# Squares, scalings and final outputs moved between engines and places in a two-layer mLSTM and attention encoder

## Chip, cores and metric

The kernel runs on one core of one Trainium2 chip. Its time is the device time of one execution in microseconds. Three runs gave a median of 1946.82 us (1946.59 to 1949.53). All tensors are float32.

## What is computed

Two sequences, a prompt of 256 tokens and a sample of 512, go through the same trunk of two layers at width 1024, each with its own conditioning vector c. In the reference, cut to what matters here:

```python
for l in range(2):
    sh1, sc1, g1, sh2, sc2, g2 = split(silu(c) @ adaln_w[l] + adaln_b[l], 6)
    h = rmsnorm(x, norm_g[l, 0]) * (1 + sc1) + sh1
    y = mlstm_mixer(h, ...) if l == 0 else swa_mixer(h, ...)
    x = x + g1 * y
    h = rmsnorm(x, norm_g[l, 1]) * (1 + sc2) + sh2
    x = x + g2 * conv_ffn(h, ...)
return rmsnorm(x, final_g)          # rmsnorm(x, g) = x * rsqrt(mean(x*x) + eps) * g

# in mlstm_mixer, for each of 4 heads (256 columns):
hs = h_fwd + h_bwd                  # two scans over the sequence, in opposite directions
hs = hs * rsqrt(mean(hs * hs, axis=-1) + eps) * head_g
```

The mLSTM projects h to queries, keys, values, output gates and 16 gate columns (an input and a forget gate for each head and direction); the attention of layer 1 looks at a window of 128 tokens to each side with a bias and a sink; the feed-forward has a convolution of width 3 and a width of 2816.

## The kernel before

**Layout.** The 768 tokens are columns: 0 to 256 the prompt, 256 to 768 the sample. The 1024 features are eight chunks of 128 partitions. A matrix product is made of three matmuls: both operands are split into a high part, rounded to the matmul's fast format, and a low part, the rest (`fp_copy_split`, L218 to L226: high part by ScalarE, low part by VectorE), and high x high, low x high and high x low are added. So each weight block `raw` that a DMA brings (five buffers) becomes `whi` and `wlo` (three buffers each), and each activation `hh` and `hl` (in the tiles `zh` and `zl`).

**Start.** `first` (L1241 on) loads the sample in two halves of 256 tokens (the first two of `RANGES`), sums squares and scales them by the root (`scaled`, L482 to L485), while PE multiplies adaLN rows to get shift and gain. When these are there, `modulate` (L487 to L494) multiplies each of the eight chunks of each half by the gain and adds the shift, in place, by a GpSimd instruction (L491), and splits it. Then `mlstm` loads the prompt and starts its norm (L576 to L579): eight squares on ScalarE (L102), all but the last two added up by GpSimd (L106), a matmul with a vector of 1/1024 on PE that sums over the partitions (L118), add and power (VectorE L120, GpSimd L123), a broadcast on PE (L128), and then, in `modulated` (L466 on), product (VectorE L474), high part (ScalarE L476) and low part (VectorE L477). Meanwhile `window` (L273 on) multiplies the gates' block and the first two query blocks with the two sample halves and then the prompt.

**Order.** The Python code states an order, in which `tick` and `step` interleave norms and adaLN work between the products; a scheduler of the framework then sets each engine's final order. An engine runs its own queue in order. From the start on, VectorE also works on layer 1's adaLN (`adaln_v`: L431, L433, on rows that come through the same five `raw` buffers).

**Gates and heads.** After the window, VectorE scans the gates over time (L590 to L597); the rows go through DRAM (L599, L615), GpSimd adds masks (L617), ScalarE takes exponentials (L676 to L680), VectorE multiplies them into the scores (L681, L682). For each head and sequence, the outputs `hs` (128 tokens x 256) are summed from two directions (L725, L726), squared with an accumulated sum (L728), the root is taken (VectorE L730, GpSimd L731), GpSimd multiplies `hs` by it (L734), PE transposes it (L738) and VectorE applies `head_g` (L742). There are 24 such blocks: 4 heads times 4 blocks of the sample and 2 of the prompt.

**End.** The last step of the second feed-forward goes over the three ranges (two halves of the sample, then the prompt). For each it makes eight output tiles of six matmuls in four rotating banks `pa`, adds each to the residual (VectorE L507), squares the result (ScalarE L102) and ticks (L1208), which lets the norm of the range before advance between the tiles. The last norm's `output` (L496 to L501) writes x times the root times `final_g` to a new tile `nt` (eight buffers, which the squares share) and starts a DMA of each chunk to the result.

Of the kernel before, what the change touches and what calls it, by code (L numbers as in the profile page):

```python
# [12 lines left out]
AF = mybir.ActivationFunctionType  # L13
ALU = mybir.AluOpType

P = 128
D = 1024
KC = D // P
# [4 lines left out]
SAMPLE, PROMPT = (256, 768, 0), (0, 256, 1)  # L23
RANGES = ((256, 512, 0), (512, 768, 0), PROMPT)
# [23 lines left out]
FG = HG + 8  # L48
# [26 lines left out]
def col(t):  # L75

    return t + (GAP if t >= 256 else 0)
# [7 lines left out]
class Norm:  # L85

    def __init__(self, net, xt, rng, apply, pool_adds=True):
        self.net, self.xt, self.rng, self.apply = net, xt, rng, apply  # L90
        self.n = rng[1] - rng[0]
        self.sums = []
        self.add = net.nc.gpsimd.tensor_tensor if pool_adds else net.nc.vector.tensor_tensor

    def x(self, c):
        return self.xt[c // 4][:, c % 4, self.rng[0] : self.rng[1]]

    def square(self, c):

        net = self.net  # L100
        sq = net.tmp([P, self.n])
        net.nc.scalar.activation(sq, self.x(c), AF.Square)  # L102
        self.sums.append(sq)
        if 2 <= len(self.sums) and self.count < KC - 2:
            acc = self.sums[0]
            self.add(acc, acc, self.sums.pop(), ALU.add)  # L106
        self.count += 1

    count = 0
# [28 lines left out]
class Net:  # L138
# [348 lines left out]
    def modulate(self, xt, rng, l, i):  # L487
        c0, c1, q = rng
        for c in range(KC):
            x = xt[c // 4][:, c % 4, c0:c1]  # L490
            self.nc.gpsimd.tensor_scalar(  # L491
                x, x, self.gain[l][i][:, c, q : q + 1], self.mod[l][:, 24 * i + c, q : q + 1], ALU.mult, ALU.add
            )
            self.fp_copy_split(self.hh[:, c, c0:c1], self.hl[:, c, c0:c1], x)  # L494

    def output(self, x, pr, rng):  # L496
        for c in range(KC):
            t = self.tmp([P, rng[1] - rng[0]])
            self.nc.vector.scalar_tensor_tensor(t, x(c), self.cst(FG + c), pr, ALU.mult, ALU.mult)  # L499
            self.nc.sync.dma_start(self.io["y"][:, c, rng[0] : rng[1]], t)  # L500
        return ()  # L501


# [45 lines left out]
    def mlstm(self, pool, gw, xt):  # L549
        nc, io = self.nc, self.io  # L550
# [22 lines left out]
        ws = [(gw, gates)] + [(w, keep(qt0, 0, c)) for c, w in self.halves(U_MIN)]  # L573
        self.load_x(io["x"], RANGES[2:], xt)
        nc.sync.dma_start(self.kct[:, P:], io["kc"][:, P : 3 * P])
        norm = Norm(self, xt, PROMPT, self.modulated(0, 0))  # L576
        for c in range(KC):
            norm.square(c)
        self.start(PROMPT, norm.stages())  # L579
# [30 lines left out]
        for h in range(4):  # L610
# [13 lines left out]
            for i in range(2):  # L624
# [3 lines left out]
                t = self.slab([P, 2, 2, T], R)  # L628
# [30 lines left out]
            for q, (s0, s1) in enumerate(SEQS):  # L659
                n = (s1 - s0) // P  # L660
                for j in range(n):
# [21 lines left out]
                    if q == 0:  # L683
                        t = [pool.tile([P, 640], R, tag="PT", name=self.nm("PT"), bufs=8) for _ in range(2)]
# [14 lines left out]
            ss = pool.tile([P, T6], F32, tag="ss", name=self.nm("ss"), bufs=2)  # L699
            for q, (s0, s1) in enumerate(SEQS):  # L700
                n = (s1 - s0) // P
                self.step(self.fillp, 2)
                hq = []
                for i in range(n):
                    ti = s0 // P + i
                    hs = pool.tile([P, 256], F32, tag="hs", name=self.nm("hs"), bufs=4)
                    hq.append(hs)
                    dn = pool.tile([P, 2], F32, tag="dn", name=self.nm("dn"), bufs=4)
                    out = []
                    for d in range(2):  # L710
                        o = self.pa()[:, :258]
                        js = range(0, i + 1) if d == 0 else range(i, n)
                        for j in js:
                            ph, pl = pts[q, j, d]
                            c0 = (i - j) * P if d == 0 else i * P
                            tj = s0 // P + j
                            self.mm(o, ph[:, c0 : c0 + P], v[:, 0, tj], j == js[0], False)
                            self.mm(o, ph[:, c0 : c0 + P], v[:, 1, tj], False, False)
                            self.mm(o, pl[:, c0 : c0 + P], v[:, 0, tj], False, j == js[-1])
                        nc.scalar.activation(dn[:, d : d + 1], o[:, 256:257], AF.Abs)  # L720
                        out.append(o)
                    em = eT[:, ti, h:36:32]
                    nc.vector.tensor_tensor(dn, dn, em, ALU.max)
                    nc.vector.reciprocal(dn, dn)
                    nc.scalar.activation(hs, out[0][:, :256], AF.Copy, scale=dn[:, 0:1])  # L725
                    nc.vector.scalar_tensor_tensor(hs, out[1][:, :256], dn[:, 1:2], hs, ALU.mult, ALU.add)  # L726
                    sq = pool.tile([P, 256], F32, tag="sq", name=self.nm("sq"), bufs=1)
                    nc.scalar.activation(sq, hs, AF.Square, accum_out=ss[:, ti : ti + 1])  # L728
                t0, t1 = s0 // P, s1 // P
                nc.vector.tensor_scalar(ss[:, t0:t1], ss[:, t0:t1], 1.0 / 256.0, EPS, ALU.mult, ALU.add)  # L730
                nc.gpsimd.tensor_tensor(ss[:, t0:t1], ss[:, t0:t1], self.mhalf[:, : t1 - t0], ALU.pow)  # L731
                for ti in range(t0, t1):
                    hs = hq[ti - t0]
                    nc.gpsimd.tensor_scalar(hs, hs, ss[:, ti : ti + 1], 1.0, ALU.mult, ALU.mult)  # L734
                for c in range(2):
                    pt = self.pa()
                    for ti in range(t0, t1):
                        nc.tensor.transpose(  # L738
                            pt[:, (ti - t0) * P : (ti - t0 + 1) * P], hq[ti - t0][:, c * P : (c + 1) * P], self.ident
                        )  # L740
                    ch = 2 * h + c
                    nc.vector.tensor_scalar(  # L742
                        hsT[ch // 4][:, ch % 4, s0:s1], pt[:, : s1 - s0], self.cst(HG + ch), None, ALU.mult
                    )
# [221 lines left out]
    def combined(self, l, i, pool):  # L966
# [20 lines left out]
        def apply(x, pr, rng):  # L987
            if rng[0] == 0:
                for c in range(KC):
                    full[c] = one(F32)  # L990
                    modulate(full[c], c, x, pr, rng)
                    put((self.B11, self.B21)[c // 4], c % 4, full[c])
                return
# [123 lines left out]
    def ffn(self, l, xt, pool, apply, keep=None):  # L1117
        nc = self.nc
# [61 lines left out]
        def down(p, g):  # L1180
            ws = (w for _, w in self.halves(u0 + 3 * p + 2))
            chunk = lambda w, i: [t[:, 512 * i : 512 * (i + 1)] for t in w]

            def tile(w, c, rng):
                s0, s1, _ = rng
                o = self.pa()[:, : s1 - s0]
                cs = slice(c % 4 * P, (c % 4 + 1) * P)
                for i in range(2):
                    wh, wl = chunk(w, i)
                    gh, gl = (g[:, z, i, col(s0) : col(s0) + s1 - s0] for z in range(2))  # L1190
                    self.mm(o, wh[:, cs], gh, i == 0, False)
                    self.mm(o, wh[:, cs], gl, False, False)
                    self.mm(o, wl[:, cs], gh, False, i == 1)
                self.resid(xt, o, l, 40, c, rng)

            if p < NPART - 1:
                for h, w in enumerate(ws):
                    for rng in SAMPLE, PROMPT:
                        for c in range(4 * h, 4 * h + 4):
                            tile(w, c, rng)  # L1200
                return
            ws = list(ws)
            for rng in RANGES:
                norm = Norm(self, xt, rng, apply)
                for c in range(KC):
                    tile(ws[c // 4], c, rng)
                    norm.square(c)
                    self.tick(0.65)  # L1208
                if keep is not None:
                    self.save_x(xt, keep, rng)  # L1210
                self.start(rng, norm.stages())

        prev = None
        for p in range(NPART):
            g = up(p)
            if prev is not None:
                down(*prev)
            prev = (p, g)
        down(*prev)


# [175 lines left out]
```

## Time and profile before

| what | us |
|---|---|
| median of three runs | 1946.82 |
| the profiled execution's own time | 1955.06 |
| its span, from the first instruction's start to the last one's end | 1953.2 |
| TensorE (PE) busy | 1851.3 |
| VectorE (DVE) busy | 1390.8 |
| ScalarE (ACT) busy | 895.8 |
| GpSimd (POOL) busy | 555.1 |

The profile is of one execution. Its page gives busy times, a chain of work followed back from the end, and the costliest groups of instructions. Further views of the trace give the waits (which line waited for which), the instructions in order of time, and the busy time of each engine in a chosen stretch with the granted TensorE clock (1.00 is full). The program's names stand for tiles; L507 is line 507 of the kernel; PEld is the weight load, which runs beside PE. An idle time in brackets behind an instruction is what its engine spent waiting before it, and what ended the wait.

### The profile page before, as it was taken

To read this page: it belongs to the slowest core of one execution; us is meant where nothing else is said; L and a number is where in the kernel's file an instruction comes from. 1 tells how busy PE (TensorE), PEld (TensorE's weight loads), DVE (VectorE), ACT (ScalarE), POOL (GpSimd) and SP (SyncE) were. 2 spreads that over 40 slices of the span, in tenths; PEclk is the share of its full clock that TensorE was granted. 3 is DMA by queue.
4 is the path that set the end of the run, shared out by engine and by line. 5 is a ranking of instruction groups with operands and counts; after the bars stand their busy time and mean duration, and the time that the engine had idled before them with its cause. 6 is when DMAs were issued, how large, how long until landed. Compare 5 with 4: busy or idle time off the path is not lost. (4 is left out here: it accounts for less than half of the span.)

```text
span 1953.2 us, 28783 instructions
## 1 busy us (share of the span) xinstructions
PE 1851.3 (95%) x11122; PEld 1673.9 (86%) x11122; DVE 1390.8 (71%) x2261; ACT 895.8 (46%) x1785; POOL 555.1 (28%) x448
## 2 busy tenths in 40 slices
PE   6799999999979999999999999999799999999997
PEld 3686887888978999999999998779789999999997
DVE  4756675684577777777777765775877777777776
ACT  3343433343446444444444555774554444444442
POOL 4203011032213333333331311342123333333323
PEclk8899999999989999999999999999899999999998
DMA  9335445455212222222222221122212222222211
GB/s 341 100 100 188 150 155 198 150 157 169 76 44 76 65 66 65 65 65 65 65 66 87 98 89 49 40 85 76 65 56 65 72 69 66 72 68 65 65 33 66
DMA packets 63381, 181.32 MB, mean 93 GB/s; under 512 B 6071, under 2 KB 23735, under 8 KB 63244
## 3 DMA queue, kind: packets, MB, share of 16 engines
q1 hardware_dynamic: 63244, 179.49, 28.7%
q8 instruction: 87, 1.43, 0.3%
q14 instruction: 50, 0.41, 0.1%
HBM read 173.03 MB, written 6.43 MB: 92 GB/s over the span
## 5 line engine op out<-in xcount | busy, mean ns | idle before, releaser
L222 ACT CAST whi<-raw 128x1024 fp32r<-128x1024 f32 x247 | 258.5, 1047 | 414.0 <-PE pa L216 202.8
L223 DVE TENSOR_TENSOR wlo<-raw,whi 128x1024 fp32r<-128x1024 f32 x247 | 330.5, 1339 | 104.1 <-ACT whi L222 103.5
L216 PE MATMUL pa<-slab,whi 128*128 128x256 f32 (+1 forms) x1472 | 349.1, 335 | 3.7 <-DVE slab L507 2.6
L216 PEld LDWEIGHTS pa<-slab,whi 128*128 128x128 f32 x1472 | 253.4, 191 | 35.3 <-DVE slab L507 9.2
L507 DVE SCALAR_TENSOR_TENSOR slab<-pa,mod,slab 128x256 f32<-128x256 f32 (+1 forms) x368 | 206.9, 591 | 59.2 <-PE pa L216 59.1
L216 PE MATMUL pa<-slab,wlo 128*128 128x256 f32 (+1 forms) x736 | 234.6, 332 | 0.0
L216 PE MATMUL ps<-zh,whi 128*128 128x256 f32 (+2 forms) x688 | 230.1, 338 | 4.6 <-ACT zh L222 2.7
L216 PE MATMUL ps<-zh,wlo 128*128 128x256 f32 (+2 forms) x688 | 229.3, 337 | 2.8 <-DVE wlo L223 2.8
L216 PE MATMUL ps<-zl,whi 128*128 128x256 f32 (+2 forms) x688 | 231.0, 338 | 0.9 <-DVE zl L477 0.7
L1040 PE MATMUL ps<-zh,whi 128*128 128x384 f32 x504 | 173.7, 345 | 20.9 <-ACT ps L1093 18.2
L1041 PE MATMUL ps<-zl,whi 128*128 128x384 f32 x504 | 171.8, 341 | 4.1 <-DVE zl L223 4.1
L1042 PE MATMUL ps<-zh,wlo 128*128 128x384 f32 x504 | 171.5, 340 | 0.0
L216 PEld LDWEIGHTS pa<-slab,wlo 128*128 128x128 f32 x736 | 140.1, 191 | 12.3
L216 PEld LDWEIGHTS ps<-zh,whi 128*128 128x128 f32 x688 | 132.8, 194 | 20.2 <-ACT zh L222 3.5
L1053 POOL TENSOR_TENSOR raw<-raw 128x512 f32<-128x512 f32 x38 | 69.0, 1815 | 284.3 <-DMA raw<-in_w_dram 132.6
L216 PEld LDWEIGHTS ps<-zh,wlo 128*128 128x128 f32 x688 | 133.4, 194 | 14.1 <-DVE wlo L223 3.4
L216 PEld LDWEIGHTS ps<-zl,whi 128*128 128x128 f32 x688 | 133.4, 194 | 12.3 <-issue 1.7
L1130 DVE SCALAR_TENSOR_TENSOR slab<-slab,cstt,slab 128x771 f32<-128x771 f32 x88 | 131.5, 1496 | 1.4
L1165 POOL TENSOR_TENSOR slab<-slab 128x772 f32<-128x772 f32 x44 | 89.5, 2035 | 139.6 <-DVE slab L1130 124.8
L1055 POOL TENSOR_TENSOR raw<-raw,raw 128x512 f32<-128x512 f32 x38 | 49.1, 1291 | 266.5 <-DVE wlo L223 245.8
L1129 DVE SCALAR_TENSOR_TENSOR slab<-slab,cstt,slab 128x771 f32<-128x771 f32 x88 | 103.0, 1172 | 29.8 <-ACT slab L1127 29.8
L1040 PEld LDWEIGHTS ps<-zh,whi 128*128 128x128 f32 x504 | 96.2, 191 | 29.9 <-ACT ps L1093 24.0
(261 smaller groups left out, 4220.1 us busy)
## 6 DMA issues: line engine op xcount, KB each, us to landing
raw<-in_w_dram SPq DMA_DIRECT2D x202, 512.0 KB, 3.7
raw<-in_adaln_w_dram SPq DMA_DIRECT2D x84, 512.0 KB, 4.3
slab<-in_x_dram SPq DMA_DIRECT2D x12, 512.0 KB, 9.1
slab<-in_adaln_w_dram SPq DMA_DIRECT2D x12, 512.0 KB, 10.2
slab<-mrows SPq DMA_DIRECT2D x8, 384.0 KB, 4.8
xs<-slab SPq DMA_DIRECT2D x6, 512.0 KB, 2.9
bt<-brow SPq DMA_DIRECT2D x16, 192.0 KB, 3.2
slab<-xs SPq DMA_DIRECT2D x6, 512.0 KB, 9.3
```

The costliest lines, as they stand in the source:

```text
L216: self.nc.tensor.matmul(out, lhsT, rhs, start=start, stop=stop)
L222: nc.scalar.copy(hi, src)
L223: nc.vector.tensor_tensor(lo, src, hi.bitcast(F32), ALU.subtract)
L507: self.nc.vector.scalar_tensor_tensor(x, o, self.mod[l][:, gc + c, q : q + 1], x, ALU.mult, ALU.add)
L1040: mm(o, wh[:, k], hi[k], start=start and k == 0, stop=False, skip_group_check=True)
L1041: mm(o, wh[:, k], lo[k], start=False, stop=False, skip_group_check=True)
L1042: mm(o, wl[:, k], hi[k], start=False, stop=k == 3, skip_group_check=True)
L1053: tt(q[2], q[2], q[3], ALU.add)
L1055: tt(q[0], q[2], q[0], ALU.subtract)
L1129: stt(y[:, 1:], u[:, :-1], w(0), y[:, 1:], ALU.mult, ALU.add)
L1130: stt(y[:, :-1], u[:, 1:], w(2), y[:, :-1], ALU.mult, ALU.add)
L1165: nc.gpsimd.tensor_tensor(y, y, yrow[:, j], ALU.mult)
```

## The change

1. `Norm` gets a number `on_pe`: so many squares at the end are summed by PE rather than added by GpSimd. It is 2 as before, and 8 for the prompt's first norm: GpSimd adds nothing there, and PE's sum goes over eight tiles instead of three.
2. `modulate` of the sample uses VectorE instead of GpSimd: 16 instructions.
3. The scaling of the head outputs by the root uses ScalarE's copy with a scale instead of GpSimd: 24 instructions.
4. `output` writes in place of x, so no `nt` tile is taken.
5. In the very last range of the second layer only the first three tiles tick, so that the norm of the range before comes as far as its root, and its outputs follow behind all eight tiles of the last range.

The new file has one line less from `output` on, so its line numbers there are lower by one.

```diff
-    def __init__(self, net, xt, rng, apply, pool_adds=True):
+    def __init__(self, net, xt, rng, apply, on_pe=2):
...
-        self.add = net.nc.gpsimd.tensor_tensor if pool_adds else net.nc.vector.tensor_tensor
+        self.on_pe = on_pe
...
-        if 2 <= len(self.sums) and self.count < KC - 2:
+        if 2 <= len(self.sums) and self.count < KC - self.on_pe:
             acc = self.sums[0]
-            self.add(acc, acc, self.sums.pop(), ALU.add)
+            net.nc.gpsimd.tensor_tensor(acc, acc, self.sums.pop(), ALU.add)
...
             x = xt[c // 4][:, c % 4, c0:c1]
-            self.nc.gpsimd.tensor_scalar(
+            self.nc.vector.tensor_scalar(
...
         for c in range(KC):
-            t = self.tmp([P, rng[1] - rng[0]])
-            self.nc.vector.scalar_tensor_tensor(t, x(c), self.cst(FG + c), pr, ALU.mult, ALU.mult)
-            self.nc.sync.dma_start(self.io["y"][:, c, rng[0] : rng[1]], t)
+            self.nc.vector.scalar_tensor_tensor(x(c), x(c), self.cst(FG + c), pr, ALU.mult, ALU.mult)
+            self.nc.sync.dma_start(self.io["y"][:, c, rng[0] : rng[1]], x(c))
...
-        norm = Norm(self, xt, PROMPT, self.modulated(0, 0))
+        norm = Norm(self, xt, PROMPT, self.modulated(0, 0), KC)
...
-                    nc.gpsimd.tensor_scalar(hs, hs, ss[:, ti : ti + 1], 1.0, ALU.mult, ALU.mult)
+                    nc.scalar.activation(hs, hs, AF.Copy, scale=ss[:, ti : ti + 1])
...
                     norm.square(c)
-                    self.tick(0.65)
+                    if keep is not None or rng is not RANGES[-1] or c < 3:
+                        self.tick(0.65)
```

## Prediction

> **What bounds the kernel now.** I read the page first: which engine has no slack.
>
> ```profile
> span 1953.2 us, 28783 instructions
> PE 1851.3 (95%) x11122; PEld 1673.9 (86%) x11122; DVE 1390.8 (71%) x2261; ACT 895.8 (46%) x1785; POOL 555.1 (28%) x448
> ```
>
> PE works 1851.3 of 1953.2 us, so a change that leaves the matmuls alone can win from two things only: PE's 102 us of idle time, and stretches in which PE runs at a lowered clock. The list of waits says who ends PE's idle time (who waits <- for whom: total us, times, longest).
>
> ```profile
> PE pa L216 <- POOL nt L106: 10.7, 6, 5.9
> PE ps L1041 <- DVE zl L223: 10.4, 5, 3.2
> PE ps L216 <- ACT nt L102: 10.1, 1, 10.1
> PE pa L738 <- POOL hs L734: 6.4, 5, 2.6
> ...
> PE pa L216 <- DVE zl L477: 4.4, 1, 4.4
> ```
>
> Three of these touch edited lines: the sum of squares (L106), the head scaling (L734), and the prompt's normalised copy (L477), which stands behind the first. The third row is the program's start, which stays. Next, the busy time by stage (stretch, its length, PE, PEld, DVE, ACT, POOL with counts, granted clock, DMA share, GB/s).
>
> ```profile
> 36.00:50.00 14.00, 12.42 (x76) 11.64 (x77) 10.66 (x21) 8.78 (x23) 13.86 (x16) 0.76 0.73 267
> 50.00:63.00 13.00, 7.08 (x42) 6.88 (x41) 10.64 (x10) 1.10 (x3) 9.57 (x7) 0.78 0.29 83
> 63.00:84.50 21.50, 16.67 (x120) 16.23 (x120) 13.18 (x23) 8.80 (x18) 0.00 (x0) 0.89 0.24 74
> 84.50:105.00 20.50, 18.63 (x110) 16.33 (x109) 19.50 (x25) 10.35 (x13) 0.00 (x0) 1.00 0.42 141
> 105.00:158.00 53.00, 52.95 (x349) 43.93 (x347) 21.02 (x49) 20.63 (x61) 11.17 (x9) 1.00 0.29 92
> ```
>
> From 105 us PE is full. Before that it is not, and its clock is low. The timeline shows why.
>
> ```profile
> 36.14 15.36 POOL L491 TENSOR_SCALAR slab<-slab,gain,mod 128x256 f32<-128x256 f32 x16 [7.34 <-DVE gain L402]
> ...
> 51.47 6.73 POOL L106 TENSOR_TENSOR nt<-nt,nt 128x256 f32<-128x256 f32 x5
> ...
> 58.26 2.72 PE L216 MATMUL pa<-inv,nt 128*128 128x2 f32 x12 [5.92 <-POOL nt L106]
> ```
>
> POOL modulates the sample for 15.36 us; the prompt's five sums queue behind it and take 6.73 us more; PE, in order, waits 5.92 us for them, and later 4.37 us for the prompt's L477. The sums take 0.74 us each in the tail but 1.35 here, and DVE's two-input L433 takes 1.69 us each here (5.06 for three) against 1.24 elsewhere (2.48 for two): the two engines slow each other.
>
> **Front part (sample on VectorE, prompt's squares on PE).** In the built instruction order all 16 scalings stand on DVE ahead of the first low half (L223), and POOL's queue holds no sum and no scaling there. The trace has no DVE tensor_scalar of 128x256 from SBUF. Lower bound: L431, the same kind at 1024 columns, 0.775 us back to back, a quarter is 0.19. Upper bound: a two-input L474, 0.40 back to back (3.22 for eight). L433 against L474 gives a fixed part of 0.12; L431 less that, over four, plus it again is 0.28. I take 0.28, nearest to the same kind: 16 x 0.28 = 4.5 us of DVE (3.0 to 6.4). PE does ten more tiny matmuls, 20 rows of the trace: 1.50 us per 12 rows at full clock, 2.72 at half, so 2.5 to 4.5 us, at 37 to 42 us, where PE waits for the low halves anyway; without that cover it is that much.
>
> Now DVE's queue in the new order, from 36.1: scalings to 40.6; seven low halves at 0.41, weight split 1.21, one low half, L431 twice, four low halves and the norm's add to about 48.6 (the sums are ready by 42); weight split, four low halves, L433 twice to 54; L474 eight times to 57.2; L433 twice, six L477, L433, two L477 to 64.2. In the trace L477 ends at 77.7. PE's 72 matmuls for the prompt (gates and two query halves) take 24 x 0.12 us for each of the last two items after that and end near 70 instead of 84.4. That lead of 14 us is not all kept: the next things in line are DVE's. Behind L477 stand four evictions, three weight splits, six L433 that the old order had earlier, one wait of some 1.6 us for an adaLN row (its buffer is freed later in this order), and the gate scans. They end near 91.5 instead of 100.5. PE then finds the key evictions of DVE not done when it wants their banks, and the mask rows, POOL's L617 and ACT's exponentials start from the scans: 9 us earlier, not 14. From there PE is full with cover on both sides (last row above), and the order of all engines is the same as before from the end of the mLSTM to the tail, so a lead is carried to the end. A check from DVE's side: from 36 to 105 it is idle 15 of 69 us (rows above); it gets 4.5 of work and loses 2.2 of interference (three L433 at 1.69 instead of 1.24, two L223 at 0.90 instead of 0.48), so -9 leaves it under 4 us of idle. **Front: -9 us** (-3 if 10 us of that idle stay, -14 if PE's lead survives whole).
>
> The Trainium skill (Perfetto Trace Analysis, Optimizing Scalar/DVE Operations) speaks against this step: with DVE saturated, work should leave it, and shifting work between GpSimd and DVE might gain nothing as they share a port. The row bears half of it out: DVE is busy 10.66 of 14 us and 19.50 of 20.5. By that rule the sum would be the first rival's.
>
> **Head outputs on ScalarE.** 24 instructions.
>
> ```profile
> 151.38 1.84 POOL L734 TENSOR_SCALAR hs<-hs,ss 128x256 f32<-128x256 f32 x4
> ...
> 167.67 3.44 POOL L734 TENSOR_SCALAR hs<-hs,ss 128x256 f32<-128x256 f32 x2
> ```
>
> Alone one takes 0.46 us; at 167.67, while DVE runs L223 and L433, 1.72. The Trainium skill (SBUF — State Buffer, Who interferes with whom) says a DVE instruction with two SBUF inputs blocks a GpSimd one that reads SBUF; these rows agree. On ACT the nearest rows are the squares of the same shape, 0.41 each, 0.33 back to back (2.62 for eight). So where POOL was undisturbed nothing is won (the 2.65 us wait at 327.95 stands behind a chain of normaliser and square that stays). At 169.75 and 171.17 PE waits 2.00 and 0.88 us: on ACT the first would be ready 0.41 after the power ends at 167.6, leaving about 0.5: -2.4. At 436.0 and 437.4 it waits 0.39 and 0.51: -0.9. The granted clock is 0.50 from 170 to 175 us and 0.82 from 175 to 180 (stages of 5 us), which costs PE 2.5 + 0.9 = 3.4 us; it follows the idle of 166.8 to 169.7, and with that nearly gone I count -2 (0 to -3.4). ACT gets 24 x 0.33 = 8 us at 46% load and stands still while the first scaling of each of eight groups waits for POOL's power (0.71 to 2.14 us); behind it stand key and query evictions and weight splits. In the trace ACT idles 6.63 and 2.77 us at two of these places, which covers it; +0.5. **Heads: -4.8 us** (+1 to -7).
>
> **Tail.** The outputs go to the residual tile itself, so a square no longer waits for an output's transfer (2.5 us, once). The eight outputs of the first half-range stand ahead of the next residual instead of between residuals: 8 x 0.40 = 3.2 us from 1926.3, so the bank for the fourth tile comes at 1929.5 instead of 1928.8, and the sum after it 0.3 later: PE +1.0. The second half-range's eight stand behind the last residual and ahead of the last norm's add (L120):
>
> ```profile
> 1942.11 0.48 DVE L507 SCALAR_TENSOR_TENSOR slab<-pa,mod,slab 128x256 f32<-128x256 f32 x1
> 1942.51 0.48 DVE L499 SCALAR_TENSOR_TENSOR nt<-slab,cstt,pa 128x256 f32<-128x256 f32 x1
> 1944.28 0.16 DVE L120 TENSOR_SCALAR nr<-pa 128x2 f32<-128x2 f32 x1 [1.29 <-PE pa L216]
> ...
> 1946.60 3.22 DVE L499 SCALAR_TENSOR_TENSOR nt<-slab,cstt,pa 128x256 f32<-128x256 f32 x8 [2.16 <-PE pa L216]
> ```
>
> PE's last tile ends at 1940.6 now. It comes at about 1940.8 then (+1.0, less 0.8 for a broadcast moved behind it); broadcast and eight outputs take 4.0; L120 at 1944.8 instead of 1944.28. The residuals gain what L120 loses. **Tail: +0.5 us** (-3 if the low clock goes, 0.66 from 1930 to 1940, which costs 3.4; +3 if L120 waits for all of the outputs and the residuals gain nothing).
>
> **Sum:** -9 - 4.8 + 0.5 = -13.3. The profiled execution took 1955.06 us (span 1953.2), 8.2 above the median 1946.82; it would become 1941.8, and the median **1933.5**. About 0.2%, 3.9 us, is what a measurement of this kernel can tell from no change.
>
> **Rivals.** (1) *DVE becomes the front's bound.* For: its load; the L433s are only moved. Against: POOL's interference goes (2.2 us of DVE). Front -3, heads half, -2.4, tail +0.5: -4.9, 1942. (2) *The waits change names and all cancels*: PE's gaps reappear as waits for low halves, banks and ACT, within 3.9 us of 1947. (3) *Slower: ACT blocked at the head of its queue.* If POOL's power is held up by DVE as at 240.29 (2.14 us), each of eight groups stops ACT about 2.5 us, 20 us in all; with no cover, and heads gaining nothing, -9 + 20 + 0.5 = +11.5: 1958. It decides from the point where more than 8.5 of the 20 us reach PE; against it are ACT's idle stretches above. (4) *More is kept*: front -14, heads -7: 1926. That the scheduler undoes the change is out: the order shows each edit.
>
> Chances: forecast (1927 to 1939) 0.58, rival 1 0.17, rival 2 0.10, rival 3 0.10, rival 4 0.05. Faster 0.80, same 0.10, slower 0.10. The range 1924 to 1944 takes in the forecast, rivals 1 and 4 and the bounds of the unknown costs.
>
> **What would show it.** Right: no PE wait on L106 near 58 us; the prompt's matmuls over by about 70; scans over near 91; PE full from about 96; no PE wait over 1 us on the heads; the tail as long as now. Wrong: DVE scalings of over 0.4 us, PE waiting for DVE where it waited for POOL, many waits of PE for ACT between 150 and 450, or a last L120 more than 3 us behind the last residual.

## The result and the profile after

Over 16 runs of each the changed kernel took 1942.9 us in the median (1939.5 to 1948.9) and the kernel before 1951.97 (1946.6 to 1955.1): ratio 0.9964, 95% interval 0.9954 to 0.9975, so 0.36% or some 7 us shorter (the ratio is estimated from all runs; the means lie 7.4 us apart, the medians 9.1). In a second measurement (e17) the ratio was 0.9958 (0.9943 to 0.9974). All 23 runs of it against all 107 of the kernel before give -7.0 us in the mean, +/- 1.6. The forecast was -13.3 us. The sign came as told; the size is half.

The profiled execution hides that. It took 1941.91 us against 1955.06 for that of before: -13.15, which is the forecast to 0.2 us. Its page, span and busy times:

```profile
span 1940.1 us, 28794 instructions
...
PE 1846.7 (95%) x11142; PEld 1672.8 (86%) x11142; DVE 1392.0 (72%) x2277; ACT 905.9 (47%) x1809; POOL 506.6 (26%) x403
```

POOL lost 48.5 us, ACT has 10 more; PE's idle time is 93 us instead of 102. The list of waits (who waits <- for whom: total, times, longest):

```profile
PE pa L216 <- ACT slab L222: 6.0, 2, 5.8
PE pa L737 <- ACT hs L733: 3.9, 2, 3.6
...
PE pa L216 <- POOL nt L106: 2.7, 4, 1.0
...
PE pa L216 <- DVE E L681: 2.1, 2, 1.6
```

L106, 10.7 us before, is down to 2.7 (the tail's), L477 with its 4.4 is gone, the heads went from 6.4 to 3.9. New is the first row, 5.8 us in one piece; the last was 0.4 (L682 there). (Lines behind the outputs count one less than in before: L733 and L737 are the old L734 and L738.) Three of the stages of the prediction, by the windows view (stretch, length, PE, PEld, DVE, ACT, POOL, granted clock, DMA share, GB/s):

```profile
50.00:63.00 13.00, 13.00 (x111) 13.00 (x111) 13.00 (x24) 5.28 (x11) 1.37 (x1) 1.00 0.43 132
63.00:84.50 21.50, 21.50 (x142) 19.74 (x141) 17.49 (x19) 11.17 (x14) 0.00 (x0) 1.00 0.50 163
84.50:105.00 20.50, 14.67 (x97) 13.49 (x96) 15.51 (x22) 7.99 (x16) 3.66 (x2) 0.83 0.34 105
```

PE and DVE are full together from 50 to 63 us, and PE at full clock to 84.5. The stage behind that, with 1.9 us of idle time at full clock before, now has 5.8 us of idle time and a low clock. The timeline shows what holds it:

```profile
36.53 5.25 DVE L491 TENSOR_SCALAR slab<-slab,gain,mod 128x256 f32<-128x256 f32 x16
...
85.92 1.22 DVE L223 TENSOR_TENSOR wlo<-raw,whi 128x1024 fp32r<-128x1024 f32 x1
...
87.17 0.33 SPq L231 DMA_DIRECT2D raw<-in_w_dram  x1
...
90.87 1.05 ACT L222 CAST whi<-raw 128x1024 fp32r<-128x1024 f32 x1 [9.89 <-DMA raw<-in_w_dram]
...
94.04 1.58 ACT L222 CAST slab<-ps 128x512 fp32r<-128x512 f32 x4
...
94.66 3.78 PE L216 MATMUL pa<-slab,slab 128*128 128x512 f32 x8 [5.83 <-ACT slab L222]
```

A low half behind the first four scans frees a raw buffer at 87.14; SP then issues the weight load, ACT stands 9.89 us idle for it, and the evictions that PE needs are queued behind it, a table load and an exponential (91.93 to 94.13) on ACT. The heads where the prediction had looked:

```profile
158.00 0.71 POOL L730 TENSOR_TENSOR ss<-ss,mhalf 128x2 f32<-128x2 f32 x1 [11.44 <-DVE ss L729]
158.74 0.91 ACT L733 ACTIVATE hs<-hs,ss 128x256 f32<-128x256 f32 x2 [0.78 <-POOL ss L730]
...
159.31 0.84 PE L737 MATMUL pa<-kct,hs 128*128 128x128 f32 x4 [0.33 <-ACT hs L733]
```

The two scalings that held PE for 2.00 and 0.88 us now hold it for 0.33. And the tail:

```profile
1927.47 0.48 DVE L506 SCALAR_TENSOR_TENSOR slab<-pa,mod,slab 128x256 f32<-128x256 f32 x1 [0.23 <-PE pa L216]
1927.98 3.22 DVE L498 SCALAR_TENSOR_TENSOR slab<-slab,cstt,pa 128x256 f32<-128x256 f32 x8
...
1931.12 0.15 DVE L120 TENSOR_SCALAR nr<-pa 128x2 f32<-128x2 f32 x1
```

L120 stands behind all eight outputs, 3.17 us after the last residual, where it was 1.69 us; from the last residual to the span's end it is 12.15 us instead of 10.6.

### The profile page after: what moved, and what is told of

It reads as the page before. It is cut to its first block, busy times and chain, and to the rows that moved or that the text cites. A ratio compares the mean times of both kernels' runs of the same rounds, so it can differ in the third digit from the quotient of the medians.

```text
span 1940.1 us, 28794 instructions
## 1 busy us (share of the span) xinstructions
PE 1846.7 (95%) x11142; PEld 1672.8 (86%) x11142; DVE 1392.0 (72%) x2277; ACT 905.9 (47%) x1809; POOL 506.6 (26%) x403
## 3 DMA queue, kind: packets, MB, share of 16 engines
HBM read 173.03 MB, written 6.43 MB: 93 GB/s over the span
## 5 line engine op out<-in xcount | busy, mean ns | idle before, releaser
L1052 POOL TENSOR_TENSOR raw<-raw 128x512 f32<-128x512 f32 x38 | 63.5, 1672 | 281.7 <-DMA raw<-in_w_dram 165.1
## 6 DMA issues: line engine op xcount, KB each, us to landing
slab<-in_adaln_w_dram SPq DMA_DIRECT2D x12, 512.0 KB, 10.2
```

The costliest lines, as they stand in the source:

```text
L1052: tt(q[2], q[2], q[3], ALU.add)
```

## Experiments

Two theories at the start. **A**: the sum was right for its trace, and the failed step is that one execution's waits and low clock were taken for typical. **B/C/D**: a part (front, heads or tail) is worth less than its term. First the kernel before again, and each part alone, the diffs against before.

**e1, before again** (no edit).

> The kernel before, unchanged, for a second trace of it. Theory A (the sum held in the trace, and the failed step is that one execution's waits and low-clock stretches were taken for typical): same time within 0.1% in the median, single executions spread over some 8 us with the granted clock, and the second trace, with the same instruction order, runs some us ahead of the first, gained in stretches where the first shows half clock (36 to 85, 91 to 105 or 165 to 178 us, or the tail), not in busy instructions at full clock. Theory B (the waits are the same in every execution, and the change loses on average what its trace does not show): the second trace has the same landmarks as the first within 2 us up to 1843.

Median 1950.97 us, ratio 1.001 (0.9996 to 1.0025). Its profiled execution is 4.8 us shorter than the first, with the same instructions in the same order. Where they differ is the granted clock. The same 30 us of the clock in three executions (last columns: clock, DMA share, GB/s; the changed kernel is some 12 us further on in the program there), before:

```profile
1080.00:1110.00 30.00, 27.65 (x214) 26.81 (x214) 22.41 (x52) 15.12 (x34) 11.03 (x13) 0.94 0.33 110
```

before again (e1):

```profile
1080.00:1110.00 30.00, 28.16 (x180) 27.32 (x179) 20.70 (x47) 14.10 (x33) 9.86 (x11) 0.78 0.26 87
```

the changed kernel:

```profile
1080.00:1110.00 30.00, 29.58 (x242) 28.60 (x243) 22.91 (x51) 17.56 (x37) 6.11 (x8) 1.00 0.26 83
```

PE does 180 matmuls in e1 where it does 242 in the changed kernel, in code that the change doesn't touch. Counted by matmuls, between the 6000th and the 6500th matmul e1 loses 4.6 us on before, the changed kernel gains 1.5. The clock record explains the step: in every trace the clock is 1.00 or 0.50, and each half-clock stretch lasts 3.4, 6.8 or 10.2 us (other lengths only at the span's end), most of them at or just behind an idle moment of PE. Summed over the span they are 83.5 us in before, 73.3 in e1, 73.1 in the changed kernel, 55.3 in e17. At half clock a 128x512 matmul of before follows the last one by 0.43 us (173.36 to 174.22) instead of 0.23 (177.01 to 177.24), so half of PE's busy time in them is lost: 33.4, 27.4, 29.6 and 19.6 us. So 4 to 6 us of the difference between before's trace and those of e1 and the changed kernel are such stretches, and theory A's first half stands. The Trainium skill (TensorE: Matmul & The Clock Gate, Part 1: The HAM clock gate) says that the clock is decided in free-running windows of 3413 ns that do not start with the kernel; the record agrees: all stretches of before start 2.70 us off a grid of 3.4133, all of e1 1.22, all of the changed kernel 3.37.

**e2, front alone**: the diff's on_pe and L491 hunks.

```diff
-            self.nc.gpsimd.tensor_scalar(
+            self.nc.vector.tensor_scalar(
...
-        norm = Norm(self, xt, PROMPT, self.modulated(0, 0))
+        norm = Norm(self, xt, PROMPT, self.modulated(0, 0), KC)
```

> The front edits alone (prompt's squares summed on PE, sample scaled on VectorE). Theory A: the trace leads before by 8 to 10 us at 330 us as the changed kernel does, the new 5.8 us wait of PE near 94.7 us is there too, and the timed difference is -5 to -8 us, most of the whole change's -7. Theory B (each part alone is worth its term, together they cost): timed -9 us. Theory C (the front is the part that pays less, since the wait at 94.7 takes its gain): timed -2 to -4 us.

Ratio 0.9976 (0.996 to 0.9992), some -5 us; PE's wait of 5.8 us is there (5.83 at 93.4). Its trace leads before by 11.1 us at 320 us.

**e3, heads alone.**

```diff
-                    nc.gpsimd.tensor_scalar(hs, hs, ss[:, ti : ti + 1], 1.0, ALU.mult, ALU.mult)
+                    nc.scalar.activation(hs, hs, AF.Copy, scale=ss[:, ti : ti + 1])
```

> The head outputs on ScalarE alone. Theory A: the waits at 169.75, 171.17, 436 and 437.4 us go (3.7 us of PE) and the low clock behind the first of them goes only in some executions; timed -1 to -3 us. Theory B: timed -4.8 us as the term had it. Theory C (ACT blocked at the head of its queue eats it): timed 0 to +3 us, with PE waits on ACT in the trace behind the scalings.

Ratio 0.9998 (0.9985 to 1.001): nothing that can be told from zero. The four waits are gone, and no wait of PE on ACT stands behind the scalings but that of the chain at 327 us (2.8 us).

**e4, tail alone**: the output and tick hunks.

```diff
-            t = self.tmp([P, rng[1] - rng[0]])
-            self.nc.vector.scalar_tensor_tensor(t, x(c), self.cst(FG + c), pr, ALU.mult, ALU.mult)
+            self.nc.vector.scalar_tensor_tensor(x(c), x(c), self.cst(FG + c), pr, ALU.mult, ALU.mult)
...
+                    if keep is not None or rng is not RANGES[-1] or c < 3:
```

> Outputs in place and behind the last residuals, alone. Theory A: timed 0 (-1 to +1.5 us), last norm's add (L120) at most 3 us later against the last residual, nothing before 1900 us differs but by the clock. Theory D (the tail is a loss that the traces hide, since the last power on GpSimd stands behind eight outputs on VectorE): timed +2 to +4 us.

Ratio 1.0016 (0.9997 to 1.0036). Inconclusive between A and D: its runs spread from 1946 to 1961.

Whole kernels are too blurred for terms of a few us, so the next four end with the mLSTM, in which front and heads lie.

**e5 to e8, cut kernels**: before, front, heads, and the changed kernel.

```diff
             act = self.first(pool)
+        for k in range(KC):
+            self.nc.sync.dma_start(self.io["y"][:, k], act(k, 0, T)[0].bitcast(F32))
+        return
```

> The kernel before up to the end of the mLSTM (some 500 us): everything behind it is left out, and the gated head outputs are written as the output, so that the 1450 us behind, with their own low-clock stretches, no longer blur the time of the edited part. Reference for the next three; its executions should spread over 2 to 4 us instead of 13 (theory A2: most of the spread comes from low-clock stretches behind 500 us) or over 8 us still (theory B2: the edited part itself varies).

> The same cut with the front edits alone. Theory A2 (the lead of 10 to 11 us that the one trace shows at 330 us is there in every execution, and is blurred later): 10 to 12 us shorter than the cut kernel before. Theory B2 (that trace was a lucky one): about 6 us shorter, as the timed difference of the whole kernels, 5 to 6 us.

> The same cut with the head outputs on ScalarE alone. If what is won at 170 us is given back at 184 to 200 us to VectorE, as one trace of it and the changed kernel's show: 1 to 2.5 us shorter (0.9 of it from the waits at 436 us). If the term of the sum holds: 4.8 us shorter.

> The same cut of the changed kernel. Theory A2: 11.5 to 13.5 us shorter than the cut kernel before. Theory B2: 7 to 8 us shorter. If front and heads get into each other's way: less than the two parts together by over 1 us.

| cut kernel | median us (range) | mean | against e5 (means) |
|---|---|---|---|
| e5 before | 478.4 (477.2 to 479.3) | 478.45 | |
| e6 front | 472.0 (469.6 to 472.1) | 471.39 | -7.1 |
| e7 heads | 475.7 (475.1 to 476.2) | 475.70 | -2.75 |
| e8 both | 468.1 (467.2 to 469.6) | 468.26 | -10.2 |

The 95% intervals of the differences are +/- 1.4, 0.8 and 1.4. The spread is 1 to 2.5 us, so most of the blur does come from behind. The parts add up (-9.85 against -10.2). Front is near the -6 of theory B2, heads a little above the 1 to 2.5 us expected, e8 between its two theories: front and heads are both short of their terms (-9, -4.8). Where they lose it is seen at markers that all kernels have, the starts of the heads' transposes (head 0's second, head 2's first and second) and the end of the last work on the gated outputs (tile sg), in us:

| kernels | head 0, second | head 2, first | head 2, second | gated outputs end |
|---|---|---|---|---|
| before, e1, e5 | 169.8, 170.9, 170.7 | 328.0, 328.2, 328.6 | 343.9, 342.7, 343.3 | 475.3, 473.5, 473.7 |
| front: e2, e6 | 159.2, 161.1 | 318.8, 321.7 | 333.4, 336.7 | 464.8, 467.4 |
| heads: e3, e7 | 169.6, 167.9 | 326.6, 326.7 | 341.5, 342.8 | 471.6, 471.6 |
| both: after, e8, e17 | 159.3, 158.5, 157.6 | 317.6, 317.8, 315.0 | 332.9, 333.2, 329.9 | 464.0, 462.5, 460.3 |

Front's mean lead is 10.3 us at head 0 and 8.0 at head 2: there PE waits 4.6 and 5.2 us for the heads (e2, e6) instead of 2.9 (e5): the chain behind that wait moved up by less than PE. With both edits the wait is 3.6 to 4.0 us, against 2.8 and 3.4 with the heads alone, so little is lost there. The heads' lead, matmul by matmul (these kernels have one order of PE): against before, e3 and e7 stand at -3.9 and -5.6 us at 184 us, and at -1.0 and -1.6 at 201. So 3 to 4 us are won and given back within 17 us. The changed kernel's traces (after, e8, e17; their matmuls matched by tiles and turn, against the mean of before, e1, e4 and e5) lead by 14.2, 14.9 and 15.8 us at 184, all that the sum had promised to there (9 + 2.4 + 2 = 13.4), by 10.8, 10.8 and 13.9 at 201, and by 11.1, 10.8 and 14.1 at 345. What PE meets there, in the timeline of e5 (SP issues weight loads):

```profile
175.98 0.33 SPq L231 DMA_DIRECT2D raw<-in_w_dram  x1
...
178.37 0.33 SPq L231 DMA_DIRECT2D raw<-in_w_dram  x1
```

and of e7, with ACT's casts of these weights and PE's next wait:

```profile
175.37 0.33 SPq L231 DMA_DIRECT2D raw<-in_w_dram  x1
...
177.76 0.33 SPq L231 DMA_DIRECT2D raw<-in_w_dram  x1
...
179.93 1.05 ACT L222 CAST whi<-raw 128x1024 fp32r<-128x1024 f32 x1 [5.36 <-DMA raw<-in_w_dram]
...
183.72 1.05 ACT L222 CAST whi<-raw 128x1024 fp32r<-128x1024 f32 x1 [2.47 <-DMA raw<-in_w_dram]
...
190.29 5.06 PE L216 MATMUL pa<-slab,slab 128*128 128x512 f32 x14 [2.14 <-DVE slab L223]
```

PE is about 5 us earlier, the loads are not (0.6 us), ACT now waits for the first of them too, and PE for what follows. In the kernel before POOL's mask adds (L617) run in the same stretch, and DVE's low half beside them takes 2.15 us (2.92 and 2.45 in e7); that was the rival cause.

**e9, e10: every second adaLN transfer left out**, in e5 and in e7.

```diff
-            if (grp, k) != rows[-1]:
+            if (grp, k) != rows[-1] and k % 2:
                 raw = fetch(*rows[grp * KC + k + 1])
```

> The cut kernel before with every second transfer of an adaLN row of the second layer left out (the row before is used twice; VectorE's work on it stays). Reference for the next one. If transfers set the pace between 173 and 200 us, the weight loads of the next head, which land at 173.0, 179.9 and 183.7 us in the cut kernel with the heads edit, land some us earlier.

> The same with the heads edit. Theory H (heads win 4 to 5.6 us at 170 us, and 2.5 to 4 of it are given back by 201 us because the next head's weight loads land at the same time as before): with fewer transfers the lead at 201 us stays 3.5 us or more, and the cut kernel is 4 to 5.5 us shorter than e9. Rival (VectorE's own work, L433 and the low halves, takes the lead, whatever the transfers do): the lead at 201 us is 1 to 1.7 us as in e7, and the cut kernel 2 to 3 us shorter than e9.

476.4 us (473.7 to 478.7) and 476.4 (475.5 to 479.1): no difference is seen (+0.4 +/- 2.3 us in the means). But both expectations missed: with fewer transfers the raw buffers are handed out in another order, and PE has no wait on the heads at 170 us in e9 either, so there was nothing to win. It tells nothing of who gives the lead back.

**e13, e14: no mask adds for the later heads**, in e5 and in e7.

```diff
-                nc.gpsimd.tensor_tensor(
+                h or nc.gpsimd.tensor_tensor(
                     mb[:, 2 + d].rearrange("p (t c) -> p t c", t=T6),
...
-                    act(E[:, j * P : nb], mb[:, 3, ks], AF.Exp, bias=ab, scale=-1.0)
-                    act(E[:, nb : nb + P], mb[:, 2, ks], AF.Exp, bias=af, scale=-1.0)
+                    act(E[:, j * P : nb], mb[:, 1 if h else 3, ks], AF.Exp, bias=ab, scale=-1.0)
+                    act(E[:, nb : nb + P], mb[:, 0 if h else 2, ks], AF.Exp, bias=af, scale=-1.0)
```

> The cut kernel before with GpSimd's mask adds (L617) left out for the three later heads, whose exponentials read the unmasked rows; the rows' transfers stay. Reference for the next one. If GpSimd's mask adds slow VectorE at 180 to 190 us, the low half at 180.84 (2.15 us in the kernel before) and the two L433 at 184.65 (1.91 each) take 1.2 each here.

> The same with the heads edit. Theory V (the lead of 4 to 5.5 us at 184 us is given back by 201 us because VectorE, slowed by GpSimd's mask adds, is late with the next head's keys): without them the lead at 201 us against e13 is 3.5 us or more. Theory H (the next head's weight loads land at the same time whatever PE does, as SP issues them when VectorE frees a raw buffer): still 1 to 2 us at 201 us, with the loads issued within 0.5 us of e13's. In both cases the cut kernel is shorter than e13 by that lead plus 0 to 1 us.

475.5 us (473.1 to 476.6) and 474.1 (472.8 to 474.5): -1.4 (means -1.3 +/- 1.7). The low half takes 1.2 us in both, as expected. e13 has no wait on the heads either, so it leads e5 by 4.8 us at 184 us by itself, and by only 1.4 at 201, with no mask add near. e14 stands 1.3 ahead of e13 there. So the lead is given back without a mask add, and theory V falls as the whole cause; whether the adds have a share (e14 gives back 2.1 us, e3 and e7 2.9 and 4.0) single traces cannot tell. The weight loads are issued at 175.22 and some 2.4 us later in e13, and at 175.08 and 177.47 in e14, within a us of e5's, as theory H has it. Whoever comes early to 173 us waits for the same loads. What paces their issue is SP's wait for a raw buffer, and e5's timeline shows who frees it:

```profile
167.20 0.33 SPq L231 DMA_DIRECT2D raw<-in_w_dram  x1
...
173.65 1.05 ACT L222 CAST whi<-raw 128x1024 fp32r<-128x1024 f32 x1 [5.92 <-DMA raw<-in_w_dram]
...
174.73 1.23 DVE L223 TENSOR_TENSOR wlo<-raw,whi 128x1024 fp32r<-128x1024 f32 x1 [1.18 <-ACT whi L222]
```

The low half of one load ends at 175.96, and the next load goes out at 175.98; the one after that follows an L433, which has read its adaLN row by 178.35. In e7 the same steps stand at 166.25, 173.03, 174.12 and 175.37. From the load at 167.20 on, the chain to the next issues runs over transfers, ACT and DVE, not over the heads that PE is early with. In the changed kernel these two loads are 9.2 us earlier than in e5, and PE over 14.

**e15, e16: one half of the front each**, cut (the diffs here are against e6): only the sample on VectorE (the prompt's sums stay on POOL), and only the sums on PE (the scaling stays on POOL).

```diff
-        norm = Norm(self, xt, PROMPT, self.modulated(0, 0), KC)
+        norm = Norm(self, xt, PROMPT, self.modulated(0, 0))
```

```diff
-            self.nc.vector.tensor_scalar(
+            self.nc.gpsimd.tensor_scalar(
```

> The cut kernel with the sample scaled on VectorE, and the prompt's squares still summed on GpSimd. If most of the front's gain comes from freeing GpSimd's queue: the sums are over by 45 us, the 5.9 us wait of PE at 58 us is gone, and it is 5 to 7 us shorter than e5. If only the PE sums matter: under 2 us shorter.

> The cut kernel with the prompt's squares summed on PE, and the sample still scaled on GpSimd. If the sums behind the scalings are what PE waits for: the wait at 58 us is gone without any work added to VectorE, and it is 5 to 7 us shorter than e5, as much as both edits together (6 to 7). If the scalings themselves set the low halves' time: under 2 us shorter.

470.6 us (469.6 to 472.2): -7.8 against e5 in the mean, as much as both together (-7.1, ranges overlap). 473.2 (472.8 to 474.1): -5.1. (e13 to e16 ran on another chip than e5; the kernel before differs by under 1 us of 1950 between them.) The first alone takes all and the second most of it, so the two are not a sum. e16's waits show why it falls short:

```profile
PE pa L216 <- ACT slab L222: 4.7, 1, 4.7
PE pa L216 <- POOL nr L123: 4.2, 1, 4.2
```

The prompt's power (L123), on POOL too, now stands behind the 16 scalings, and PE waits 4.2 us for it at 53.6.

**e11, e12: the tail by itself**, the last layer with three of eleven FFN parts, before and with the tail edits.

```diff
-            act = self.first(pool)
+        act = lambda k, s0, s1: (ho[k // 2][:, 0, k % 2, s0:s1], ho[k // 2][:, 1, k % 2, s0:s1])
...
-        for p in range(NPART):
+        for p in (0, 1, NPART - 1):
```

> Only the last layer's output projection and three of its eleven FFN parts, with the final norm and outputs of the kernel before: mLSTM, attention, the first layer and eight FFN parts are left out, their inputs replaced by constants. Reference for the next one; the tail should look as in the whole kernel (last residual to end some 13 us), and executions should spread over less than 4 us.

> The same with the tail edits (outputs in place, the first outputs kept behind the last residuals). Theory A: +0.5 us as the term had it (-1 to +1.5). Theory D (the tail costs more on average than the traces showed, as the spread of e4 suggests): +2 to +4 us.

278.3 us (277.6 to 279.2) and 279.2 (278.0 to 280.0): +0.8 in the mean (+/- 1.2). Theory D falls here; the term was +0.5.

**e17, the changed kernel again; e18, it without the early adaLN rows.**

```diff
         self.window(ws)
-        self.step(self.fill)
...
-                        if q <= c or h > 1:
+                        if h and (q <= c or h > 1):
```

> The changed kernel, whole, once more. By the cut pieces (front and heads together -10.2 us, tail +0.9) it should be 8 to 10 us shorter than before (-0.42 to -0.5%); if the 1450 us behind the mLSTM take part of the lead away, 5 to 7 us again (-0.25 to -0.36%). Single traces may stand anywhere from -5 to -16 against one of before, as the low-clock stretches fall.

> The changed kernel with the second layer's first four adaLN rows not asked for until the first head's values (nothing is left out: later calls take them). Theory: the 5.8 us wait of PE at 94.7 us stands behind the weight load that SP issues at 87.2 us when VectorE frees a raw buffer behind eight L433 (10 us of VectorE) and the scans; without these rows the scans are over at 80 to 84 instead of 91.9, the wait is under 2 us and the low clock behind it (6.8 us at half) goes: lead at 106 us 4 to 9 us more than the changed kernel's, of which 2 to 6 us are left at the end. Rival (the lead is given back at 180 to 200 and 318 us like that of the heads): 0 to 1.5 us left.

e17: 1942.1 us (1936.0 to 1948.6), ratio 0.9958, -8.2 us (-11.1 to -5.1). Pieces (-10.2 + 0.8) and whole agree within its interval. e18: 1947.5 (1941.4 to 1954.1), ratio 0.9981 (0.9966 to 0.9995): worse than the changed kernel by 5 us, outside of what either theory had. Its wait at 94.7 us is gone (no idle of PE over 0.5 us from 36 to 140), the scans are over at 84.2, and at 105 us it leads before by 16.9 us, the changed kernel and e17 by 5.8 and 7.4. But by 150 us it has done 677 matmuls outside of adaLN, they 670 and 685: head 0's first transposes, for which PE now waits 3.1 us, come at 144.3 us, only 1 to 2.7 before e17 and the changed kernel, and the gated outputs end at 468.2, 4 to 8 us after them. From 36 us to there PE idles less (17.1 against 19.4 and 20.3 us) and is busy longer (415.1 against 404.9 and 407.7). Lower clock explains 2.6 to 4.4 of that; PE's adaLN matmuls take 29.4 instead of 25.3 us. The built order of PE's instructions differs too, and the rest stays open. No version here beats the changed kernel.

## Why the prediction was wrong in size, point by point

- **The front's mechanism: right.** L491 took 0.33 us each (0.28 forecast, at most 0.40), no wait on L106 stands near 58, the prompt's matmuls end at 71.7 (70), the scans at 91.9 (91.5). The Trainium skill (Perfetto Trace Analysis, Optimizing Scalar/DVE Operations) says that with DVE saturated it may make sense to move work off it. Here the opposite paid: e15, which moves the 16 scalings from GpSimd to DVE, is 7.8 us shorter.
- **"so a lead is carried to the end": failed.** This is the step. The row of 105 to 158 us showed cover for 53 us, and the forecast read it as cover for good. The changed kernel's three traces lead by 14.2 to 15.8 us at 184 us and by 10.8 to 13.9 at 201: 1.9 to 4.1 us are given back there. Alone, front's lead is 10.3 us at head 0, more than the 9 forecast, 8.0 at head 2 and -7.1 in the cut times: PE runs into the heads' chain at 318 us. The new 5.8 us wait, which the forecast had merely as late key evictions, on DVE, is the first such place.
- **Heads -4.8: mis-sized, by the same step.** The waits of 2.4 and the clock of 2 us at 170 went as told (3.9 to 5.6 us ahead at 184), and most of it was given back by 201 to weight loads that are not earlier. Measured -2.75 in the cut, and nothing that can be told from zero in the whole kernel. The forecast had no row of the stretch behind 180 us in it. (Its 3.4 us for the clock from 170 to 180 us is 3.0: PE was busy only 4.12 of the first 5.) Rival 3 (ACT blocked) did not come: the heads are no loss in the cut.
- **Rival 1 (DVE becomes the front's bound) comes near in time, not by its sum.** Its -4.9 is nearer to -7.0 than the forecast, and its -2.4 for the heads is near the -2.75. But its front was -3, against -7.1: DVE is full from 36 to 63 us (13.89 of 14 and 13.00 of 13), and PE has no idle time from 50 to 84.5.
- **Tail +0.5: right within the error** (+0.8 +/- 1.2 in e12), through more time behind the last residual and less in front of it. One of the signs of being wrong came all the same, L120 more than 3 us behind the last residual (3.17).
- **Signs of being right.** Two did not come: PE is not full behind 96 us (51.01 of 53 us from 105 to 158, where it was 52.95), and it waits 3.6 us for the heads at 317.
- **"and the median 1933.5": failed too.** The profiled execution was taken as 8.2 us above the median and its savings carried over whole. It was near the upper end of its own kernel (107 runs: mean 1950.3, 1942.2 to 1958.9), and part of its excess was low-clock stretches that other executions do not have at the same place (33.4 us of PE's time against 29.6, so 3.8 of the 13.15). The base was low too: the three runs behind 1946.82 lie 3.5 us under that mean. That the two profiled executions differ by the forecast is luck: the pieces measure -7.1 - 2.75 + 0.8 = -9.05, +/- 2.
- The sum -13.3 against -9.05 in pieces is 1.9 from the front, 2.05 from the heads, 0.3 from the tail. The last 2 us, to -7.0 +/- 1.6, cannot be told from the spread of the runs.

## What to carry to other kernels

A lead won at one place is worth what the next tight place lets through: follow it past the stretch with cover to the next chain or transfer that PE does not set, and look whether that moves too. Before a trace's waits and low-clock stretches are priced, take a second trace of the same kernel; here two executions of one program differed by 4.8 us. Where terms are a few us of 1950, cut the kernel behind the edited part: the standard deviation of the runs fell from 3.0 us (before) to 0.4 to 1.2 (e5 to e8), and the terms could be measured one by one.

## What the runs showed of the hardware

- PE's clock had two values in every trace, 1.00 and 0.50, in steps of 3.4 us; the sum of the half-clock stretches of one program ran from 55.3 to 73.1 us in two executions.
- A tensor_scalar of 128x256 on VectorE with two per-partition scalars took 0.33 us back to back.
- The same power on POOL, 128x2, took 0.71 us in one place and 3.29 in another, where DVE ran full beside it. In the changed kernel:

```profile
48.08 3.29 POOL L123 TENSOR_TENSOR nr<-nr,mhalf 128x2 f32<-128x2 f32 x1 [18.55 <-DVE nr L120]
...
1931.35 0.71 POOL L123 TENSOR_TENSOR nr<-nr,mhalf 128x2 f32<-128x2 f32 x1 [3.32 <-DVE nr L120]
```
